# Output projection and its norm in the scheduler's order with sums in PSUM, and the last pair's convolution beside the first tiles of the down projection

## The chip, the cores and the metric

The kernel runs on one core of a Trainium2 chip. The metric is the device time of one execution in microseconds (us), median of several runs. Five engines work side by side: TensorE (PE, matmuls), VectorE (DVE), ScalarE (ACT), GpSimd (POOL), and SyncE (SP), whose queue issues most of the DMAs. Each engine works through its own instructions in order. An instruction waits until what it reads is there and what it overwrites is no longer needed.

## The reference, cut to what matters

The program is two transformer blocks on 1024 positions of width 1024, in float32. The second block is the one that the change touches:

```python
o = concat(rmsnorm_2(o_fox, fox_out_g), rmsnorm_2(o_sb, sb_out_g))   # two attentions, 512 columns each
x = x + o @ w_out
h = rmsnorm_2(x, ffn_norm_g)
u = causal_dwconv(h @ w_up, conv_w, conv_b)      # 3 taps along the positions, 2 * 2816 columns
gate, val = split(u, 2)
x = x + (silu(gate) * val) @ w_down
return rmsnorm_2(x, final_norm_g)
```

The norms are a mean of squares over the width and a reciprocal square root.

## The kernel before

Everything lies transposed: features on the 128 partitions, positions along the free dimension. A tile of the hidden state, `x2[ct]`, is 128 features by 1024 positions, with `ct` from 0 to 7. Positions are handled in two halves of 512, called A (the later half, `slice(HALF, L)`) and B.

**Matrix products.** Each float32 product is made of three products of rounded parts (`mm3`, lines 254 to 256: low by high, high by low, high by high). A weight tile is loaded into `wraw` (two buffers), ACT casts it to its high part `whi` (line 199), and POOL subtracts the two to give the low part `wlo` (line 190). `whi` and `wlo` have four buffers each. An activation is split the same way (`T` in the up projection, `rh` and `rl` in the down projection).

**Output projection.** After the attention (its loop ends at line 1123) the PSUM pool is opened anew with four banks `pp` of 128x512 and two double banks `cv` of 128x1024. The fox half of the product was added earlier, during the second attention (`x<-x,t` on POOL, `x<-xr,vec,ra` on DVE, `xr` loaded by SP). What is left is the product with the second attention's output `oh`, `ol`, four tiles of k. For `ct` 0 to 2 the products of k 0 to 2 go first, for both halves, since they don't need the last head pair; then the norm of the attention output (`half_rstd`, a matmul with `ones` and `rstd`, four DVE and two ACT instructions a half, result `rs`); then k 3. For `ct` 3 to 7 the twelve matmuls of a result go at once, all of half A first, then all of half B. `out_result` multiplies a sum by `rs`, adds it to `x2[ct]`, stores that to `x2_d`, squares it on ACT, and adds the square to `acc`. When the last A result is in, `half_rstd` gives the factor of the FFN norm for half A (`R3`); half B's follows later.

**Up projection.** It is a seven-product scheme (n from 1 to 7) on sums and differences of the four quarters of `x2` (`t_norm`, `t_sum`, `t_parts`) and of the weights (`up_sum`, `up_parts`), for 22 pairs `q` of a gate tile and a value tile. `order` lists the products; at step 1 the norm of half B is made, and `prep` puts the quarter's preparation on steps 1 to 8. `up_result` adds the products up on DVE. A pair's convolution (`up_rest(q, i)`, i from 0 to 6: two ACT instructions that start it in PSUM, four taps and two multiplications on DVE, a sigmoid on ACT) is spread over the seven products of the next pair. Its result goes to `f_d[q]` in memory. For the last pair all seven steps stand behind the last product.

**Down projection.** The pool is closed and opened with eight banks `pp`. Per group of two pairs the gated rows come back from `f_d` (`gated`, `load_split`), the weights `w_dn` are loaded in four tiles (`load_down`), and `down` adds two halves for each of eight `x2[ct]`, six matmuls a half. The `x2` tiles are reloaded from `x2_d` before the first group.

**What sets the order.** The Tile framework's scheduler orders each engine's instructions, except for those issued while `pinned[0]` is true: these keep the order in which the code is written. Pinned is everything from the start of the output projection (line 1131) to the end of the last pair's convolution.

Of the kernel before, what the change touches and what calls it, by code (L numbers as in the profile page):

```python
# [13 lines left out]
AF = mybir.ActivationFunctionType  # L14
# [83 lines left out]
def fused_blocks(ctx, tc, io, out, dbg=None):  # L98
# [126 lines left out]

    def rstd(total, r, n, scale=1.0 / D):

        v = ht("rv")[:, :n]
        t = ht("rt")[:, :n]
        pin(nc.vector.tensor_scalar(v, total, scale, EPS, op0=ALU.mult, op1=ALU.add))  # L230
        act(t, v, AF.Ln)
        act(r, t, AF.Exp, scale=-0.5)
        tt(t, r, r, ALU.mult)
        stt(t, t, -0.5, v, ALU.mult, ALU.mult)
        stt(r, t, 1.5, r, ALU.add, ALU.mult)

# [567 lines left out]
    def load_split(src, scale=None, lo=None):  # L804
        raw, hi, lo_ = ld("raw"), b1k("rh", F32R), b1k("rl", F32R)
        nc.sync.dma_start(raw, src)
        split(raw, hi, lo_, lo, scale)
        return hi, lo_
# [316 lines left out]


    log_exp_table(state["sig"])
    es.close()
    es = ExitStack()
    get = psum_pool(es, pp=(HALF, 4), cv=(L, 2))  # L1130
    pinned[0] = True
    A, B = slice(HALF, L), slice(0, HALF)
    rs["sb"], acc, R3 = b1k("rs"), b1k("acc3"), b1k("R3")

    def half_rstd(src, half, ps, r, scale):
        pin(nc.tensor.matmul(ps, ones, src[:, half], start=True, stop=True))
        rstd(ps, r[:, half], HALF, scale)

# [5 lines left out]
    def out_result(ct, half, ps):  # L1144
        x, t = x2[ct][:, half], ht("t")
        tt(t, ps, rs["sb"][:, half], ALU.mult)
        tt(x, x, t, ALU.add)
        dma(x2_d[ct][:, half], x)
        if ct == 0:
            act(acc[:, half], x, AF.Square)  # L1150
        else:
            sq = ht("sq")
            act(sq, x, AF.Square)
            tt(acc[:, half], acc[:, half], sq, ALU.add)

# [122 lines left out]
    def up_rest(q, i):  # L1278
# [16 lines left out]
        else:  # L1295
            tt(outs[q, 0], outs[q, 0], cv[q, 1], ALU.mult)
            dma(f_d[q], outs[q, 0])

    def out_load(ct):
        return load(io["w_out2"][ct, 1], 4, P)  # L1300
# [8 lines left out]
    for half in (A, B):  # L1309
        half_rstd(acc_o["sb"], half, wide[:, half], rs["sb"], 1.0 / 512)  # L1310
    for i, half in enumerate((A, B)):
# [6 lines left out]
    ws = [out_load(ct) for ct, _ in todo[:2]]  # L1318
    total = None
    for n, (ct, half) in enumerate(todo):  # L1320
        ps = get("pp")
        out_product(ps, ws[n], half, range(4))
        if n + 2 < len(todo):
            ws.append(out_load(todo[n + 2][0]))
        out_result(ct, half, ps)
        if n == 4:
            total = get("cv")
            half_rstd(acc, A, total[:, A], R3, 1.0 / D)
            for q in range(2):
                up_load(q)  # L1330
        elif n > 5:
            for k in (2 * (n - 6), 2 * (n - 6) + 1):
                t_norm(k, A)
                t_parts(1 + k // 4, k % 4)
    order = [(q, n) for n in EARLY for q in range(2)] + [(q, n) for q in range(2, NFF) for n in SEVEN]
    for q, n in order[:3]:
        up_parts(q, n)
    prep = {
        1: [(t_norm, j, B) for j in range(4)] + [(t_sum, 5, j) for j in range(4)], 2: [(t_parts, 5, j) for j in range(4)],
# [3 lines left out]
        8: [f for j in range(2, 4) for f in ((t_sum, 4, j), (t_parts, 4, j))],  # L1343
    }
    for s, (q, n) in enumerate(order):
        i = s % 7
        if s == 1:
            half_rstd(acc, B, total[:, B], R3, 1.0 / D)
        if s:
            up_result(*order[s - 1])  # L1350
        for f, *a in prep.get(s, ()):
            f(*a)
        if s == 8:
            up_load(2)
        elif q > 1 and i == 0 and q + 1 < NFF:
            up_load(q + 1)
        if i == 3 and s > 7:
            up_sum(q + 1 if q > 1 else 2, 6)
        if s + 4 < len(order):
            up_sum(*order[s + 4])  # L1360
        if s + 3 < len(order):
            up_parts(*order[s + 3])
        if q > 2:
            up_rest(q - 1, i)
        elif s >= 13:
            for i_ in ((0, 1), (2, 3), (4, 5), (6,))[(s - 13) % 4]:
                up_rest((s - 13) // 4, i_)
        up_product(q, n)
    up_result(*order[-1])
    for i in range(7):  # L1370
        up_rest(NFF - 1, i)
    pinned[0] = False
# [4 lines left out]
    get = psum_pool(es, pp=(HALF, 8))  # L1377

    def gated(grp):
        return unzip([load_split(f_d[2 * grp + kk], lo=nc.gpsimd) for kk in range(2)])  # L1380

    def down(grp, wd, c2, fh, fl, ranges=XH):
        for cc in range(2):
            ct = 2 * c2 + cc
            for ps, a, b in gemm([wd], fh, fl, ranges, c0=cc * P, per=2, ks=range(2)):
                tt(x2[ct][:, a:b], x2[ct][:, a:b], ps, ALU.add)

    def load_down(grp, c2):
        return load(io["w_dn"][grp, c2], 2, DV)

    f = gated(0)
    for ct in range(KD):
        x2[ct] = b1k("x2")
        nc.sync.dma_start(x2[ct], x2_d[ct])
    for grp in range(NFF // 2 - 1):
        nf = gated(grp + 1)
# [163 lines left out]
```

## Time and profile before

| | us |
|---|---|
| median of 3 runs | 2703.79 (2700.62 to 2707.94) |
| the profiled execution, its own time | 2703.25 |
| its span in the trace | 2701.5 |
| TensorE busy | 2507.0 (93%) |
| VectorE busy | 1614.9 (60%) |
| ScalarE busy | 1028.7 (38%) |
| GpSimd busy | 903.6 (33%) |

The page cuts the span into 40 slices of 67.5 us and gives each engine's busy share in tenths. A slice in which PE shows 5 or 6 is one in which the engine that does nearly all the work stands still for a third of the time or more. The granted clock (PEclk) is 9 or 10 tenths of full speed nearly everywhere. Where it is lower, the matmuls in that stretch ran partly at half speed. The waits list names, for an engine, which other engine's instruction ended each idle time.

### The profile page before, as it was taken

The numbers are of one execution on the slowest core, as the hardware profiler recorded it, in microseconds if no ns is written. First come the engines' busy times: TensorE is split into PE (matmuls) and PEld (weight loads), VectorE is DVE, ScalarE is ACT, GpSimd is POOL, SyncE is SP. The second block draws the span as 40 slices with busy tenths as digits, with TensorE's granted clock in tenths as the row PEclk, the third lists the DMA queues.
The fourth block names the chain that finished last, engine by engine and source line by source line (L and its number), as shares of the span: only waits on it lengthen the run. The fifth ranks groups of instructions, "written<-read, shape, count | busy, mean of one in ns | idle before, by whom it ended". The sixth has DMA issues, their size and how long they took to land. (4 is left out here: it accounts for less than half of the span.)

```text
span 2701.5 us, 36571 instructions
## 1 busy us (share of the span) xinstructions
PE 2507.0 (93%) x14126; PEld 1975.9 (73%) x14126; DVE 1614.9 (60%) x2351; ACT 1028.7 (38%) x1779; POOL 903.6 (33%) x671
## 2 busy tenths in 40 slices
PE   6989999999999999998999999996569999989996
PEld 3878968778787888877777666664347888878885
DVE  6363392766827132355666677785678777774446
ACT  4342262544634322333333434432234444453113
POOL 1433121211212224435332222231255444456423
PEclk9989999999999999999999999997789999999998
DMA  6423242433325553326444332420302222245212
GB/s 254 125 77 112 82 165 70 157 119 138 107 70 188 182 190 94 118 95 181 124 128 123 101 86 88 147 63 24 132 29 75 81 78 86 73 146 192 71 47 74
DMA packets 119629, 303.34 MB, mean 112 GB/s; under 512 B 14768, under 2 KB 19760, under 8 KB 119456
## 3 DMA queue, kind: packets, MB, share of 16 engines
q1 hardware_dynamic: 112160, 277.68, 31.0%
q0 software_dynamic: 7296, 23.34, 3.7%
q8 instruction: 111, 1.82, 0.3%
q14 instruction: 62, 0.51, 0.1%
HBM read 209.44 MB, written 87.29 MB: 110 GB/s over the span
## 5 line engine op out<-in xcount | busy, mean ns | idle before, releaser
L190 POOL TENSOR_TENSOR wlo<-wraw,whi 128x512 fp32r<-128x512 f32 (+1 forms) x280 | 414.5, 1483 | 1376.9 <-ACT whi L199 1321.6
L199 ACT CAST whi<-wraw 128x512 fp32r<-128x512 f32 (+1 forms) x280 | 172.2, 616 | 511.3 <-PE pp L256 380.7
L254 PE MATMUL pp<-hl,whi 128*128 128x512 f32 (+1 forms) x768 | 311.7, 406 | 4.4 <-DVE hl L193 4.4
L255 PE MATMUL pp<-hh,wlo 128*128 128x512 f32 (+1 forms) x768 | 306.9, 400 | 0.4 <-POOL wlo L190 0.4
L256 PE MATMUL pp<-hh,whi 128*128 128x512 f32 (+1 forms) x768 | 305.9, 398 | 0.0
L254 PE MATMUL pp<-rl,whi 128*128 128x512 f32 (+1 forms) x688 | 269.8, 392 | 7.0 <-DVE o L190 7.0
L254 PE MATMUL pp<-T,whi 128*128 128x512 f32 x616 | 246.8, 401 | 26.8 <-ACT whi L199 10.1
L256 PE MATMUL pp<-rh,whi 128*128 128x512 f32 (+1 forms) x688 | 269.7, 392 | 0.0
L255 PE MATMUL pp<-rh,wlo 128*128 128x512 f32 (+1 forms) x688 | 268.9, 391 | 0.0
L255 PE MATMUL pp<-T,wlo 128*128 128x512 f32 x616 | 246.1, 400 | 2.2 <-POOL wlo L190 2.2
L256 PE MATMUL pp<-T,whi 128*128 128x512 f32 x616 | 244.6, 397 | 0.0
L190 DVE TENSOR_TENSOR x<-x,pp 128x512 f32<-128x512 f32 (+1 forms) x184 | 121.7, 664 | 121.2 <-PE pp L256 121.2
L254 PEld LDWEIGHTS pp<-hl,whi 128*128 128x128 f32 (+1 forms) x768 | 144.7, 188 | 42.0 <-DVE hl L193 5.3
L255 PEld LDWEIGHTS pp<-hh,wlo 128*128 128x128 f32 (+1 forms) x768 | 144.6, 188 | 38.9 <-issue 6.1
L256 PEld LDWEIGHTS pp<-hh,whi 128*128 128x128 f32 (+1 forms) x768 | 144.6, 188 | 33.5 <-issue 0.4
L254 PEld LDWEIGHTS pp<-T,whi 128*128 128x128 f32 x616 | 117.3, 190 | 58.9 <-DVE T L190 11.6
L254 PEld LDWEIGHTS pp<-rl,whi 128*128 128x128 f32 x688 | 130.1, 189 | 37.1 <-issue 9.3
L190 POOL TENSOR_TENSOR wlo<-w,whi 128x512 fp32r<-128x512 f32 x88 | 115.9, 1319 | 122.4 <-ACT whi L199 122.3
L1048 DVE COPY pt<-pg 128x512 f32<-128x512 f32 (+2 forms) x192 | 101.0, 553 | 91.7 <-PE pg L1046 91.0
L256 PEld LDWEIGHTS pp<-rh,whi 128*128 128x128 f32 x688 | 130.0, 189 | 29.5 <-issue 1.7
L255 PEld LDWEIGHTS pp<-rh,wlo 128*128 128x128 f32 x688 | 130.0, 189 | 29.5 <-issue 1.3
L255 PEld LDWEIGHTS pp<-T,wlo 128*128 128x128 f32 x616 | 117.5, 191 | 30.5 <-POOL wlo L190 3.4
(380 smaller groups left out, 5515.2 us busy)
## 6 DMA issues: line engine op xcount, KB each, us to landing
w<-in_w_up SPq DMA_DIRECT2D x88, 256.0 KB
wraw<-in_w_qk SPq DMA_DIRECT2D x48, 256.0 KB
wm<-in_w_mod SPq DMA_DIRECT2D x24, 512.0 KB
wraw<-in_w_dn SPq DMA_DIRECT2D x44, 256.0 KB
f_d<-o SPq DMA_DIRECT2D x22, 512.0 KB
raw<-f_d SPq DMA_DIRECT2D x22, 512.0 KB
wraw<-in_w_out SPq DMA_DIRECT2D x37, 256.0 KB
x<-in_xT SPq DMA_DIRECT2D x16, 512.0 KB
```

Source lines behind the costliest of these rows:

```text
L190: return pin((eng or nc.vector).tensor_tensor(out=o, in0=a, in1=b, op=op))
L199: return pin(nc.scalar.copy(o, x))
L254: pin(nc.tensor.matmul(ps, ah, bl, start=first, stop=False, skip_group_check=again))
L255: pin(nc.tensor.matmul(ps, al, bh, start=False, stop=False, skip_group_check=again))
L256: pin(nc.tensor.matmul(ps, ah, bh, start=False, stop=last, skip_group_check=again))
L1048: nc.vector.tensor_copy(o, ps[:, :w])
```

## The change

1. `pinned` is set after the first three weight splits of the up projection instead of before the output projection, so the output projection, the attention's norm, the A half of the FFN norm and the preparation of half A are ordered by the scheduler.
2. `out_result` works in PSUM: the sum is multiplied by `rs` in place in its bank, and `x2` adds the bank. The squares' sum is kept in `R3`, now a double bank `cv`, instead of `acc3` in SBUF. `x2_rstd` copies half of it to SBUF (ACT), multiplies with `ones` into a `pp` bank and writes the factor back into `R3`, from which `t_norm` reads it.
3. The pinned region goes on into the down projection. At 6 products from the end the gated rows of the first two pairs are loaded and split, at 3, 2 and 1 from the end the weight tiles 0 to 2 of group 0, at 4 to 1 the `x2` tiles. Group 0's products then run in the same PSUM pool (four banks), with one step of the last pair's convolution behind each of the first seven `x2` tiles. After group 0 the eight-bank pool opens for the rest.
4. `load_split` issues its load through the helper `dma`, which can be pinned.

```diff
-    def rstd(total, r, n, scale=1.0 / D):
+    def rstd(total, r, n, scale=1.0 / D, o=None):
...
-        stt(r, t, 1.5, r, ALU.add, ALU.mult)
+        stt(r if o is None else o, t, 1.5, r, ALU.add, ALU.mult)
...
-        nc.sync.dma_start(raw, src)
+        dma(raw, src)
...
-    pinned[0] = True
...
+    def x2_rstd(half):
+
+        t = ht("acc")
+        copy(t, R3[:, half])
+        half_rstd(t, get("pp"), t, 1.0 / D, R3[:, half])
...
     def out_result(ct, half, ps):
-        x, t = x2[ct][:, half], ht("t")
-        tt(t, ps, rs["sb"][:, half], ALU.mult)
-        tt(x, x, t, ALU.add)
+        x = x2[ct][:, half]
+        tt(ps, ps, rs["sb"][:, half], ALU.mult)
+        tt(x, x, ps, ALU.add)
         dma(x2_d[ct][:, half], x)
         if ct == 0:
-            act(acc[:, half], x, AF.Square)
+            act(R3[:, half], x, AF.Square)
         else:
             sq = ht("sq")
             act(sq, x, AF.Square)
-            tt(acc[:, half], acc[:, half], sq, ALU.add)
+            tt(R3[:, half], R3[:, half], sq, ALU.add)
...
     for q, n in order[:3]:
         up_parts(q, n)
+
+    pinned[0] = True
...
         if s == 1:
-            half_rstd(acc, B, total[:, B], R3, 1.0 / D)
+            x2_rstd(B)
...
         up_product(q, n)
+        left = len(order) - s
+        if left == 6:
+            f = gated(0)
+        elif left < 4:
+            wd.append(load_down(0, 3 - left))
+        if left < 5:
+            x2_load(8 - 2 * left)
+            x2_load(9 - 2 * left)
     up_result(*order[-1])
-    for i in range(7):
-        up_rest(NFF - 1, i)
+    wd.append(load_down(0, 3))
+    for c2 in range(4):
+        down(0, wd[c2], c2, *f, step=lambda n: up_rest(NFF - 1, n) if n < 7 else None)
     pinned[0] = False
```

The order that results is read from the two built programs. On POOL, at the end of the attention, `x` are the sums with the fox half and `wlo` the low parts of the output weights. Before:

```order
L190 TENSOR_TENSOR x_2916_15972<-x_2916_15972,t_15973 128x512 x2
L190 TENSOR_TENSOR x_2943_16096<-x_2943_16096,t_16097 128x512 x2
L190 TENSOR_TENSOR x_2965_16179<-x_2965_16179,t_16180 128x512 x2
L190 TENSOR_TENSOR wlo_16229<-wraw_16227,whi_16228 128x512
L190 TENSOR_TENSOR wlo_16235<-wraw_16233,whi_16234 128x512
L190 TENSOR_TENSOR wlo_16241<-wraw_16239,whi_16240 128x512
L190 TENSOR_TENSOR wlo_16381<-wraw_16379,whi_16380 128x512
```

And after:

```order
L190 TENSOR_TENSOR wlo_16233<-wraw_16231,whi_16232 128x512
L190 TENSOR_TENSOR x_2886_15833<-x_2886_15833,t_15834 128x512 x2
L190 TENSOR_TENSOR wlo_16239<-wraw_16237,whi_16238 128x512
L190 TENSOR_TENSOR x_2916_15972<-x_2916_15972,t_15973 128x512 x2
L190 TENSOR_TENSOR wlo_16374<-wraw_16372,whi_16373 128x512
L190 TENSOR_TENSOR x_2943_16096<-x_2943_16096,t_16097 128x512 x2
L190 TENSOR_TENSOR x_2965_16179<-x_2965_16179,t_16180 128x512 x2
L190 TENSOR_TENSOR wlo_16380<-wraw_16378,whi_16379 128x512
```

The low parts of the first four output weight tiles (one more of them stands ahead of the rows shown) now stand between the attention's sums; before, the first of them stood behind the last sum. Their four casts on ACT moved in the same way, from behind the attention's last `oh` into the attention.

On DVE, the first results of the output projection (`t` and `pp` a sum times `rs`, `x` the hidden state, `acc` and `cv_16321` the sum of squares, `cv_16243` the sum of the third tile). Before:

```order
L190 TENSOR_TENSOR t_16341<-pp_16246,rs_16224 128x512
L190 TENSOR_TENSOR x_2764_15298<-x_2764_15298,t_16341 128x512
L190 TENSOR_TENSOR t_16346<-pp_16248,rs_16224 128x512
L190 TENSOR_TENSOR x_2794_15431<-x_2794_15431,t_16346 128x512
L190 TENSOR_TENSOR acc_2974_16225<-acc_2974_16225,sq_16350 128x512
L190 TENSOR_TENSOR t_16353<-cv_16245,rs_16224 128x512
L190 TENSOR_TENSOR x_2829_15570<-x_2829_15570,t_16353 128x512
L190 TENSOR_TENSOR acc_2974_16225<-acc_2974_16225,sq_16357 128x512
```

And after:

```order
L190 TENSOR_TENSOR pp_16244<-pp_16244,rs_16224 128x512
L193 SCALAR_TENSOR_TENSOR rs_16224<-rt_16314,rs_16224 128x512
L190 TENSOR_TENSOR x_2764_15298<-x_2764_15298,pp_16244 128x512
L190 TENSOR_TENSOR pp_16246<-pp_16246,rs_16224 128x512
L190 TENSOR_TENSOR cv_16243<-cv_16243,rs_16224 128x512
L190 TENSOR_TENSOR x_2794_15431<-x_2794_15431,pp_16246 128x512
L190 TENSOR_TENSOR x_2829_15570<-x_2829_15570,cv_16243 128x512
L190 TENSOR_TENSOR pp_16245<-pp_16245,rs_16224 128x512
L190 TENSOR_TENSOR cv_16321<-cv_16321,sq_16347 128x512
L190 TENSOR_TENSOR x_2764_15298<-x_2764_15298,pp_16245 128x512
L190 TENSOR_TENSOR cv_16321<-cv_16321,sq_16353 128x512
```

The addition of a square no longer stands right behind the result that it comes from, but one or two results later; and half B's first results stand among half A's.

On DVE, at the end of the up projection (`o` is a row of the last pair, `cv` its convolution, `x` with `pp` a sum of the down projection). Before:

```order
L190 TENSOR_TENSOR o_19996<-u_19957,pp_19999 128x512
L193 SCALAR_TENSOR_TENSOR cv_20042<-o_19976,vec,cv_20042 128x1023
L193 SCALAR_TENSOR_TENSOR cv_20042<-o_19976,vec,cv_20042 128x1022
L193 SCALAR_TENSOR_TENSOR cv_20044<-o_19996,vec,cv_20044 128x1023
L193 SCALAR_TENSOR_TENSOR cv_20044<-o_19996,vec,cv_20044 128x1022
L190 TENSOR_TENSOR o_19976<-o_19976,cv_20042 128x1024
L190 TENSOR_TENSOR o_19976<-o_19976,cv_20044 128x1024
L190 TENSOR_TENSOR x_3677_20071<-x_3677_20071,pp_20105 128x512
```

And after:

```order
L190 TENSOR_TENSOR o_20000<-u_19957,pp_20003 128x512
L190 TENSOR_TENSOR x_3658_19996<-x_3658_19996,pp_20082 128x512
L190 TENSOR_TENSOR x_3658_19996<-x_3658_19996,pp_20090 128x512
L190 TENSOR_TENSOR x_3659_19998<-x_3659_19998,pp_20100 128x512
L190 TENSOR_TENSOR x_3659_19998<-x_3659_19998,pp_20108 128x512
L193 SCALAR_TENSOR_TENSOR cv_20098<-o_19976,vec,cv_20098 128x1023
L190 TENSOR_TENSOR x_3665_20022<-x_3665_20022,pp_20119 128x512
L190 TENSOR_TENSOR x_3665_20022<-x_3665_20022,pp_20127 128x512
L193 SCALAR_TENSOR_TENSOR cv_20098<-o_19976,vec,cv_20098 128x1022
```

The six convolution steps that stood in a row ahead of the first down sum now stand one by one behind pairs of down sums.

## Rows read from the trace of the kernel before

**Rows 1.** The page: busy tenths in 40 slices, PE and its granted clock.

```profile
PE   6989999999999999998999999996569999989996
...
PEclk9989999999999999999999999997789999999998
```

**Rows 2.** PE's waits, 1835 to 2030 us: total, times, longest.

```profile
PE pp L254 <- ACT whi L199: 33.8, 4, 18.8
PE pp L255 <- POOL wlo L190: 11.9, 7, 5.2
...
PE cv L1136 <- DVE acc L190: 5.0, 1, 5.0
```

**Rows 3.** Stretches of 25 us: PE, PEld, DVE, ACT, POOL busy, PEclk, DMA share, GB/s.

```profile
1850.00:1875.00 25.00, 14.71 (x52) 10.53 (x51) 5.45 (x7) 6.72 (x12) 6.21 (x5) 0.63 0.03 11
1875.00:1900.00 25.00, 9.98 (x39) 6.84 (x37) 15.09 (x23) 5.67 (x9) 0.00 (x0) 0.78 0.14 52
...
1925.00:1950.00 25.00, 17.14 (x54) 12.00 (x55) 16.54 (x21) 7.82 (x13) 7.23 (x5) 0.80 0.50 170
1950.00:1975.00 25.00, 13.17 (x36) 9.05 (x35) 12.56 (x19) 8.63 (x15) 10.13 (x7) 0.65 0.21 72
1975.00:2000.00 25.00, 15.46 (x53) 11.75 (x53) 24.90 (x27) 11.24 (x21) 14.41 (x9) 0.83 0.00 0
2000.00:2025.00 25.00, 18.52 (x67) 13.17 (x66) 21.48 (x23) 8.84 (x16) 17.20 (x12) 0.90 0.07 22
```

**Rows 4.** Timeline, PE: start, us, instruction, [idle before <- releaser]; the projection's start.

```profile
1853.68 1.70 PE L1057 MATMUL pg<-pt,vt 128*64 128x128 f32 x6
1858.64 0.79 PE L254 MATMUL pp<-ol,whi 128*128 128x512 f32 x1 [3.25 <-ACT whi L199]
1864.59 0.79 PE L255 MATMUL pp<-oh,wlo 128*128 128x512 f32 x1 [5.15 <-POOL wlo L190]
...
1878.64 1.02 PE L1136 MATMUL cv<-acc_o,ones 128*128 128x512 f32 x2
```

**Rows 5.** Timeline, PE: tile 3 A, the norms of A and B, first up product.

```profile
1904.55 0.80 PE L254 MATMUL pp<-ol,whi 128*128 128x512 f32 x1 [18.79 <-ACT whi L199]
...
1928.05 2.07 PE L1136 MATMUL cv<-acc,ones 128*128 128x512 f32 x2 [5.04 <-DVE acc L190]
...
1963.73 0.79 PE L254 MATMUL pp<-T,whi 128*128 128x512 f32 x1 [10.11 <-ACT whi L199]
...
1970.96 1.02 PE L1136 MATMUL cv<-acc,ones 128*128 128x512 f32 x2
```

**Rows 6.** Timeline, DVE: the first factor `rs`, then results.

```profile
1883.20 0.69 DVE L193 SCALAR_TENSOR_TENSOR rs<-rt,rs 128x512 f32<-128x512 f32 x1
...
1887.92 0.68 DVE L190 TENSOR_TENSOR t<-pp,rs 128x512 f32<-128x512 f32 x1
...
1891.35 0.69 DVE L190 TENSOR_TENSOR acc<-acc,sq 128x512 f32<-128x512 f32 x1 [0.69 <-ACT sq L196]
...
1916.26 1.33 DVE L190 TENSOR_TENSOR acc<-acc,sq 128x512 f32<-128x512 f32 x1 [1.77 <-ACT sq L196]
```

**Rows 7.** Timeline, ACT: the cast that releases tile 3 A.

```profile
1903.88 1.25 ACT L199 CAST whi<-wraw 128x512 fp32r<-128x512 f32 x2 [2.98 <-DMA wraw<-in_w_out]
```

**Rows 8.** End of the attention: timelines of POOL and DVE, and a group of 1810 to 1856.

```profile
1797.87 4.61 POOL L190 TENSOR_TENSOR x<-x,t 128x512 f32<-128x512 f32 x2 [8.64 <-DVE x L193]
...
1799.56 1.79 DVE L190 TENSOR_TENSOR sm<-sm,sl 128x767 f32<-128x767 f32 x1
...
L190 DVE TENSOR_TENSOR sm<-sm,sl 128x767 f32<-128x767 f32 x1 | 0.9, 942 | 0.0
```

**Rows 9.** End of the up projection: timelines of PE and DVE.

```profile
2428.93 0.76 PE L254 MATMUL pp<-rl,whi 128*128 128x512 f32 x1 [7.03 <-DVE o L190]
...
2434.61 0.58 PE L255 MATMUL pp<-rh,wlo 128*128 128x512 f32 x1
...
2422.54 5.12 DVE L193 SCALAR_TENSOR_TENSOR cv<-o,vec,cv 128x1023 f32<-128x1023 f32 x4
```

More of the change, by code (lines that the diff above doesn't have):

```diff
@@ L1130, in fused_blocks, with half_rstd @@
     get = psum_pool(es, pp=(HALF, 4), cv=(L, 2))
-    pinned[0] = True
     A, B = slice(HALF, L), slice(0, HALF)
[L1133 to L1137, printed above, removed]
+    rs["sb"] = b1k("rs")
+    def half_rstd(src, ps, r, scale, o=None):
+        pin(nc.tensor.matmul(ps, ones, src, start=True, stop=True))
+        rstd(ps, r, HALF, scale, o)
+    def x2_rstd(half):
+        t = ht("acc")
+        copy(t, R3[:, half])
+        half_rstd(t, get("pp"), t, 1.0 / D, R3[:, half])
     def out_product(bank, w, half, ks):
@@ L1297, in up_rest, with gated, down, load_down @@
             dma(f_d[q], outs[q, 0])
+    def gated(grp):
+        return unzip([load_split(f_d[2 * grp + kk], lo=nc.gpsimd) for kk in range(2)])
+    def down(grp, wd, c2, fh, fl, ranges=XH, step=None):
+        for cc in range(2):
+            ct = 2 * c2 + cc
+            for ps, a, b in gemm([wd], fh, fl, ranges, c0=cc * P, per=2, ks=range(2)):
+                tt(x2[ct][:, a:b], x2[ct][:, a:b], ps, ALU.add)
+            if step:
+                step(ct)
+    def load_down(grp, c2):
+        return load(io["w_dn"][grp, c2], 2, DV)
+    def x2_load(ct):
+        x2[ct] = b1k("x2")
+        dma(x2[ct], x2_d[ct])
     def out_load(ct):
@@ L1309, in fused_blocks @@
     for half in (A, B):
-        half_rstd(acc_o["sb"], half, wide[:, half], rs["sb"], 1.0 / 512)
+        half_rstd(acc_o["sb"][:, half], wide[:, half], rs["sb"][:, half], 1.0 / 512)
+    R3 = get("cv")
     for i, half in enumerate((A, B)):
@@ L1318, in fused_blocks @@
     ws = [out_load(ct) for ct, _ in todo[:2]]
-    total = None
     for n, (ct, half) in enumerate(todo):
@@ L1326, in fused_blocks @@
         if n == 4:
-            total = get("cv")
-            half_rstd(acc, A, total[:, A], R3, 1.0 / D)
+            x2_rstd(A)
             for q in range(2):
@@ L1344, in fused_blocks @@
     }
+    wd = []
     for s, (q, n) in enumerate(order):
@@ L1377, in fused_blocks @@
     get = psum_pool(es, pp=(HALF, 8))
[L1379 to L1395, printed above, removed]
+    f = gated(1)
+    for grp in range(1, NFF // 2 - 1):
         nf = gated(grp + 1)
```

## The prediction

> **What bounds the kernel now.** I read the page's slices first: PE shows 9 tenths nearly all the way, and in the middle, after the attention, "6 5 6" with a granted clock of 7 and 8 tenths [rows 1]. This is the only long hole that the change touches. The table of stretches then shows what kind of hole it is [rows 3]. From 1850 to 1975 us PE is busy 10 to 17 of 25 us, but DVE only 5.5 to 16.5, and ACT and POOL less: no engine is full, so the time goes into waiting for one another. From 1975 to 2025 DVE is full (24.90, then 21.48 of 25). That part is bound by DVE's work, and is not made shorter by starting anything earlier in it. The waits list names the waits [rows 2]: 33.8 us for casts of weights on ACT, 11.9 us for their low parts on POOL, 5.0 us for the squares' sum. The timeline places them: 3.25 and 5.15 us at the projection's start [rows 4], 18.79 us before tile 3 of half A and 10.11 us before the first up product [rows 5]. A second, small hole is the end of the up projection: one wait of 7.03 us [rows 9].
>
> **Output projection, in steps of when something happens.** I carry the change through four events.
>
> Start. The attention's last matmuls end at 1853.68 + 1.70 = 1855.4. Before, PE then waited for a cast (3.25) and a low part (5.15) that stood behind the attention's last work on ACT and POOL [rows 4]. In the new order both stand inside the attention, so these 8.4 us go; I take 8.0, since a bank has still to be emptied. The norm's matmul moves from 1878.64 to 1870.6 [rows 4]. The first `rs` was ready at 1883.20 + 0.69 = 1883.9 [rows 6]; it would be at 1875.9, but two DVE instructions of half B now stand ahead of it (2 x 0.69), so 1877.3.
>
> Tile 3 A. Before, it started at 1904.55 after 18.79 us [rows 5], because its cast came at 1903.88, after a DMA [rows 7] whose place in SP's queue was behind the six stores of the first results. Now its weight is loaded and cast in the attention. What it needs next is a bank, free after some three DVE instructions: 1877.3 + 2.1 = 1879.4. That is 25 us earlier.
>
> Norm of half A. PE took from 1904.55 to 1928.05 - 5.04 = 1923.0 for the five A tiles, waits included, so 18.5 us; from 1879.4 it is done by 1897.9. DVE, from 1877.3: one instruction of half B's `rs`, 8 results of 2, 7 additions of squares, and ahead of the norm 3 results of half B (6) and 2 additions: 32 x 0.69 = 22.1, so 1899.4. DVE ends last. The waits on ACT's square that each result had before (0.69 [rows 6]) are filled, because the additions come later in the queue. With the new copy on ACT (one 128x512, as long as the square: about 0.63) the norm's matmul comes at 1900.0 instead of 1928.05: 28.0 us earlier.
>
> Norm of half B. Before it came 1970.96 - 1928.05 = 42.9 us after A's [rows 5], with PE waiting 10.11 in one place. DVE was busy 16.54 + 12.56 = 29.1 us in the 50 us around it [rows 3], so some 27 to 28 in the interval itself. I take DVE as the bound now: 28. Norm B then comes at 1928.0 instead of 1970.96: **43.0 us earlier**. If nothing is gained in this interval it is 28.0.
>
> After that. The preparation behind norm B is the stretch in which DVE was full [rows 3]. Its work stays, so I give it no gain. The 8 products of `x` with the factor now read PSUM; the row shows 1.33 instead of 0.69 us for a DVE instruction on SBUF while POOL worked, 0.68 for one that reads PSUM [rows 6]. Shedding such stretches might give back 0 to 5 us (8 x 0.64), and the second copy costs 0.6: I take 0, and leave 5 for the low end.
>
> [...]
>
> **What the moved casts cost.** Four casts on ACT and four low parts on POOL now lie in the attention's end, where DVE sets the pace. While POOL was busy from 1797.87 to 1802.48, DVE's 128x767 subtraction took 1.79 instead of 0.94 us [rows 8]. Each POOL instruction may stretch one such: 4 x 0.85 = 3.4 us. A cast may also wait for one of four buffers and hold up ACT's exponentials by as much again, so 0 to 7. I take 2, since POOL's new work is short beside the sums that it does there anyway, and many of DVE's instructions there read PSUM.
>
> **End of the up projection.** Removed: the wait of 7.03 us, and the slow restart. [...] That is 14 x 0.22 = 3.1 us, 10.1 in all. The conv's work on DVE stays: four taps took 5.12, 1.28 each [rows 9]. Behind a tile's two sums (0.69 each) one step makes 2.66 us of DVE for each 12 matmuls of 12 x 0.22 = 2.6 us. That is balanced to the tenth, with only four banks between them, and the first steps wait on ACT behind casts of weights that are still loading. So I expect some of the gain to be lost: 8 of 10.1, with 0 to 10 as ends. SP is passed too: eight loads of `x2`, four of gated rows and three weight tiles move ahead of the last up products, where PE needs nothing that is not already there.
>
> **Sum.** -43 + 0 + 2 - 8 = -49 against the profiled execution's 2703.25 (its span is 2701.5, and it lies 0.5 below the median of 2703.79): **2654 us**.
>
> **Rivals.**
>
> The interval between the norms doesn't shrink. DVE's preparation of half A, which before fell into DVE's idle time (20.9 of 50 us [rows 3]), now competes with half B's results, and the weights' loads, each behind a store of a result, keep their pace. Then only 28 of the 43 us come: 2654 + 15 = 2669. For it: POOL's and ACT's links are in the way as well, and two weight buffers allow no long lead. Against it: DVE was 42% idle in that interval.
>
> The boundary gives nothing: the third and fourth weight tile of group 0 wait in SP's queue behind the store of a gated row, their casts hold back the last conv on ACT, and DVE, in order, holds the sums and the four banks. The wait of 7.03 moves a few microseconds on, with its slow restart: 2654 + 8 = 2662. Both rivals together: 2677.
>
> Slower: the attention's end stalls in SP's queue. The last two loads of `xr` now stand behind weight loads, each of which waits until POOL has freed a weight buffer, and POOL's low parts stand behind sums that wait for DVE. An `xr` that comes late stops DVE, and with it every later row of the attention, one for one. It costs more than the rest brings from 51 us of delay on; with 60 it is 2712. Against it: ACT and POOL wait there most of the time (POOL 8.64 us in the row shown [rows 8]), so the buffers come free early, and nothing near 51 us is in sight.
>
> **Chances.** The forecast (2640 to 2660) 0.55; the interval 0.22; the boundary 0.12; both 0.05; slower 0.03; some smaller cost that eats nearly all, within 8 us of before, 0.03. A measurement of this kernel tells about 0.3% (8 us) from no change. Faster: 0.55 + 0.22 + 0.12 + 0.05 = 0.94, of which I give 0.02 to the same, as I have not seen the new order's waits. So 0.92, 0.05, 0.03. The range: the low end is 2654 less 5 (stretches shed), 2 (no cost in the attention), 2 (the whole boundary) and 5 for matmuls of 1950 to 2000 that now run at 0.65 and 0.83 of the clock [rows 3]: 2640. The upper end takes in both rivals: 2679. What is left out is about 0.1.
>
> **What would show it.** Right: the norm of half A some 28 us and that of half B some 43 us earlier than their distance from the attention's end was before (72.7 and 115.6 us after 1855.4), PE's waits for casts there down from 33.8 to under 10 us, no waits of PE longer than 3 us around the first down tile. DVE should be near full from the first result to the end of the preparation. Wrong: an attention that ends later by more than 5 us; a new wait of PE for a weight's DMA between the norms; or DVE's stretch of over 20 of 25 us lasting longer than before, which would mean that its work grew.

## The result and the profile after

The changed kernel takes 2657.16 us (median of 4 runs, 2653.52 to 2660.02), the kernel before 2705.57 on the same chip. The ratio is 0.9823, with a 95% interval of 0.9803 to 0.9842: 48 us less. The prediction was 2654.

The page of the changed kernel, busy tenths in 40 slices of 66.4 us (answers to [rows 1]):

```profile
PE   5989999999999999999999999998879999999996
...
PEclk9989999999999999999999999998889999999998
```

Where PE showed "6 5 6", it shows "8 8 7", and the granted clock there is 8, 8, 8 instead of 7, 7, 8 tenths. The same hole in stretches of 25 us (columns as in [rows 3]):

```profile
1850.00:1875.00 25.00, 20.39 (x82) 15.27 (x81) 9.14 (x13) 6.58 (x13) 3.15 (x3) 0.70 0.17 55
1875.00:1900.00 25.00, 20.25 (x73) 15.16 (x71) 19.89 (x29) 10.06 (x17) 8.13 (x6) 0.86 0.33 105
1900.00:1925.00 25.00, 20.32 (x77) 15.48 (x76) 17.63 (x29) 10.72 (x18) 8.78 (x7) 0.86 0.34 116
1925.00:1950.00 25.00, 15.71 (x51) 10.49 (x49) 22.95 (x31) 12.18 (x21) 11.54 (x8) 0.86 0.18 63
1950.00:1975.00 25.00, 19.22 (x58) 13.21 (x59) 22.29 (x25) 11.34 (x20) 18.68 (x12) 0.80 0.03 7
```

PE is busy 16 to 20 of 25 us where it was busy 10 to 17, and DVE 9 to 23 where it was busy 5 to 17. Both do the same work in fewer stretches. PE's waits from 1790 to 2000 us (total, times, longest; answers to [rows 2]):

```profile
PE pg L1046 <- DVE sm L190: 12.5, 6, 5.8
PE pp L1134 <- ACT acc L199: 9.0, 2, 4.7
...
PE pp L254 <- DVE x L190: 4.7, 1, 4.7
PE pp L255 <- POOL wlo L190: 3.0, 3, 2.0
```

The waits for casts of weights (33.8 us) are gone and those for their low parts are down from 11.9 to 3.0. At the top stand waits of the attention, of which this window holds more than that of [rows 2]. Behind them stands a new one: 9.0 us for the new copies on ACT, ahead of the two matmuls of the FFN norm.

Ahead of the output projection the two traces are already 3.2 us apart, in work that the change does not touch (1.5 at their first matmul, 3.1 after 174 us). So events are compared from a common mark: the group of twelve attention matmuls below, which all kernels run alike (before, then after).

```profile
1666.70 1.09 PE L1057 MATMUL pg<-pt,vt 128*64 128x128 f32 x12
```

```profile
1669.89 1.09 PE L1057 MATMUL pg<-pt,vt 128*64 128x128 f32 x12
```

The events themselves, in PE's timeline of the changed kernel: the attention's last matmuls, its norm, tile 3 A, the norms of halves A and B, the last up matmul (answers to [rows 4, 5]):

```profile
1859.56 1.70 PE L1057 MATMUL pg<-pt,vt 128*64 128x128 f32 x6
1875.44 1.02 PE L1134 MATMUL cv<-acc_o,ones 128*128 128x512 f32 x2
1886.38 0.79 PE L254 MATMUL pp<-ol,whi 128*128 128x512 f32 x1 [4.75 <-DVE x L190]
1907.83 2.07 PE L1134 MATMUL pp<-acc,ones 128*128 128x512 f32 x2 [4.68 <-ACT acc L199]
...
1934.39 2.08 PE L1134 MATMUL pp<-acc,ones 128*128 128x512 f32 x2 [4.30 <-ACT acc L199]
...
2384.24 0.40 PE L256 MATMUL pp<-T,whi 128*128 128x512 f32 x1
```

| us after the mark | before | after | moved | predicted |
|---|---|---|---|---|
| attention's end | 188.7 | 191.4 | +2.7 | +2 |
| attention's norm | 211.9 | 205.6 | -6.4 | -8 + 2 |
| tile 3 A | 237.9 | 216.5 | -21.4 | -25 + 2 |
| norm of half A | 261.4 | 237.9 | -23.4 | -28 + 2 |
| norm of half B | 304.3 | 264.5 | -39.8 | -43 + 2 |
| last up matmul | 754.8 | 714.4 | -40.4 | -43 + 2 |
| end of the span | 1034.8 | 985.7 | -49.1 | -49 |

### The profile page after: what moved, and what is told of

The parts are those of the page before. It is cut to its first block, busy times and chain, and to the rows that moved or that the text cites. A ratio compares the mean times of both kernels' runs of the same rounds, so it can differ in the third digit from the quotient of the medians.

```text
span 2655.6 us, 36554 instructions
## 1 busy us (share of the span) xinstructions
PE 2502.2 (94%) x14126; PEld 1972.9 (74%) x14126; DVE 1607.1 (61%) x2351; ACT 1028.6 (39%) x1781; POOL 905.4 (34%) x671
## 5 line engine op out<-in xcount | busy, mean ns | idle before, releaser
L190 DVE TENSOR_TENSOR x<-x,pp 128x512 f32<-128x512 f32 (+1 forms) x198 | 130.5, 664 | 110.3 <-PE pp L256 110.3
```

The lines of the kernel that those rows point to most:

```text
L190: return pin((eng or nc.vector).tensor_tensor(out=o, in0=a, in1=b, op=op))
```

## The experiments

The question was which part of the change makes which part of the 48 us, and whether the reasons hold: the order and the waits that it removes, against the sums in PSUM, which make DVE's work shorter. Ratios are to the kernel before on the same chip, with their 95% interval. From the traces I use distances from the mark: the traces of the changed kernel, of the run without part 3 and of the run without B's products agree in them to 0.2 us up to norm B.

**The boundary alone.** The kernel before with part 3:

```diff
+        left = len(order) - s
+        if left == 6:
+            f = gated(0)
...
-    for i in range(7):
-        up_rest(NFF - 1, i)
+    wd.append(load_down(0, 3))
+    for c2 in range(4):
+        down(0, wd[c2], c2, *f, step=lambda n: up_rest(NFF - 1, n) if n < 7 else None)
```

> The kernel before with part 3 of the change alone (down projection of group 0 in the pinned region, the last pair's convolution spread over it). Theory (the parts are separate, and this one removes the 7.0 us wait and the restart at half clock): 9 us less than before, no wait of PE over 1 us at the first down products, the output projection as before. Rival (the boundary's gain needs the earlier, denser stage): within 3 us of before.

Measured: 2697.41 us, ratio 0.9970 (0.9959 to 0.9981), 8 us less. PE's only wait around the first down products is 0.9 us. The part stands by itself.

**The projection alone.** The change without part 3:

```diff
...
-    wd.append(load_down(0, 3))
-    for c2 in range(4):
-        down(0, wd[c2], c2, *f, step=lambda n: up_rest(NFF - 1, n) if n < 7 else None)
+    for i in range(7):
+        up_rest(NFF - 1, i)
```

> The whole change but part 3: the end of the up projection as in the kernel before. Theory: 40 us less than before, the wait of 7 us at the first down products back, then 3 us of slow matmuls. Rival: more than 45 us less, if the new pinned region holds something back.

Measured: 2667.62 us, ratio 0.9855 (0.9839 to 0.9871), 39 us less, and the wait of 7.0 us is back. 8 and 39 make 47: the parts add up.

**Sums in SBUF.** The change with results, squares' sums and factor in SBUF, no copy:

```diff
-        tt(ps, ps, rs["sb"][:, half], ALU.mult)
-        tt(x, x, ps, ALU.add)
+        tt(t, ps, rs["sb"][:, half], ALU.mult)
+        tt(x, x, t, ALU.add)
...
-            tt(R3[:, half], R3[:, half], sq, ALU.add)
+            tt(acc[:, half], acc[:, half], sq, ALU.add)
```

> The whole change, but results, sums of squares and the FFN norm's factor in SBUF as in the kernel before (no copy on ACT either). Theory (the order makes the gain, PSUM only spares DVE the stretching beside POOL): 0 to 5 us slower than the changed kernel, so 43 to 49 less than before. Rival (the sums in PSUM make the gain, since DVE is the bound): 20 us or more slower than the changed kernel.

Measured: 2666.08 us, ratio 0.9850 (0.9827 to 0.9874). That is 7 us slower than the changed kernel by the ratios, whose intervals overlap, and 9 by the medians: more than the theory's 0 to 5, far from the rival's 20. In the traces it is 7.8 from the attention's norm to the last up matmul, of which 6.8 lie ahead of the norm of half A. From the attention's norm to the norm of half A it takes 39.2 us instead of 32.4. The groups of DVE's instructions in that stretch show why. First the run with sums in SBUF, then the changed kernel (busy us, mean ns, idle before):

```profile
L190 DVE TENSOR_TENSOR x<-x,t 128x512 f32<-128x512 f32 x11 | 13.4, 1216 | 0.1
L190 DVE TENSOR_TENSOR acc<-acc,sq 128x512 f32<-128x512 f32 x9 | 7.2, 801 | 2.9 <-ACT sq L196 2.6
```

```profile
L190 DVE TENSOR_TENSOR cv<-cv,sq 128x512 f32<-128x512 f32 x9 | 6.3, 695 | 3.0 <-ACT sq L196 2.8
...
L190 DVE TENSOR_TENSOR x<-x,pp 128x512 f32<-128x512 f32 x9 | 6.0, 676 | 0.0
L193 DVE SCALAR_TENSOR_TENSOR rs<-rt,rs 128x512 f32<-128x512 f32 x2 | 2.4, 1224 | 0.0
L193 DVE SCALAR_TENSOR_TENSOR rt<-rt,rv 128x512 f32<-128x512 f32 x2 | 2.4, 1219 | 0.0
```

The same addition takes 1216 ns with both inputs in SBUF and 676 with one in PSUM. Eleven times 0.54 is 5.9 of the 6.8 us; the nine additions of squares (801 against 695 ns) make another 0.9.

**The old order with sums in PSUM.** The changed kernel, the projection pinned again:

```diff
     get = psum_pool(es, pp=(HALF, 4), cv=(L, 2))
+    pinned[0] = True
```

> The whole change, but the output projection pinned to the order of the code as in the kernel before; sums in PSUM, new boundary. Theory (the order makes the gain): 9 us less than before from the boundary and 0 to 5 from PSUM, so 9 to 14 less; the waits for casts (18.8 and 10.1 us) still there. Rival (PSUM makes the gain): 30 or more less than before.

Measured: 2691.56 us, ratio 0.9948 (0.9931 to 0.9966), 14 us less than before. The boundary alone gave 8, which leaves 6 for PSUM, but the intervals of the two runs overlap, and the trace shows less: the last up matmul comes 3.0 us earlier than in the kernel before. The wait before tile 3 is still there, with 18.30 us. So the order is worth the other 34, and the sums in PSUM some 3 us in the old order and 8 in the new one, by the traces.

**The start alone.** The kernel before, with the first three tiles' weights and products of k 0 to 2 left to the scheduler, by setting `pinned` behind them.

> The kernel before, with only the weights and the products (k 0 to 2) of the first three output tiles left to the scheduler, the rest pinned as before. Theory (the start's two waits, 8.4 us, go, and the attention's end pays 2 to 3 for the moved casts and low parts): 6 us less than before; the attention's norm 6 us earlier, the wait of 18.8 us before tile 3 unchanged. Rival (the attention's later end is not from the moved casts): 8 us less.

Measured: 2697.66 us, ratio 0.9974 (0.9961 to 0.9986), 7 us less. The attention ends 1.5 later, its norm comes 8.5 earlier, tile 3 still waits 18.58 us for its cast, and the last up matmul is 8.0 earlier: the start's gain is passed on whole. The time does not separate the theory's 6 from the rival's 8. That the moved tiles do cost the attention time is shown in the section on the prediction.

**The change without its start.** The changed kernel, that first part pinned:

```diff
+    pinned[0] = True
     three = [out_load(ct) for ct in range(3)]
...
             out_product(b, w, half, range(3))
+    pinned[0] = False
```

> The whole change, but the same first part pinned in the order of the code, so that the four casts and low parts stand behind the attention again. Theory: the attention ends 2.7 us earlier than in the changed kernel, PE waits 8 us more at the start, so 6 us slower than the changed kernel, 42 less than before. Rival (a later start is hidden, since DVE is the bound behind it): same as the changed kernel within 2 us.

Measured: 2662.98 us, ratio 0.9850 (0.9832 to 0.9867), 6 us slower than the changed kernel by the medians and 7 by the ratios, near the theory's 6. The norm of the attention comes 6.8 us later and the last up matmul 7.0: a later start isn't hidden.

**Without the copy.** The last addition of a half's squares writes to SBUF:

```diff
-        t = ht("acc")
-        copy(t, R3[:, half])
+        t = last[half.start]
...
+            if ct == KD - 1:
+                o = last[half.start] = ht("acc")
```

> The whole change, but the last addition of a half's squares writes to SBUF, so ACT's copy goes. PE waited 4.7 and 4.3 us for the copies. Theory (DVE's last addition ends only some 1.4 us before the matmul, so the copy is worth its own time and one hand-over): both norms 1 to 1.5 us earlier, 2 to 3 us faster than the changed kernel. Rival (the copy is the wait): 9 us faster.

Measured: 2652.00 us, ratio 0.9808 (0.9792 to 0.9824), 4 to 5 us faster than the changed kernel. From the attention's norm to the last up matmul the trace gains 3.0 us, which is the theory's 2 to 3. Its parts are others: the norm of half A comes 1.2 us earlier from there, as forecast, but the interval between the norms shrinks by 3.4, and 1.5 of that are lost again behind norm B. Another 2.6 us of the trace lie before the attention's norm, where the order is the same; the paragraph on the clock below tells of them. The rival is out: PE's wait of 4.7 us before norm A only changed its name, to 4.05 for DVE's addition. That of 4.3 before norm B fell to 1.0, since the copy for B stood on ACT behind two casts and began 2.0 us after its input was there, as ACT's and DVE's rows of the changed kernel show:

```profile
1932.57 1.28 ACT L199 CAST T<-x 128x512 fp32r<-128x512 f32 x2 [1.49 <-DVE x L193]
1933.76 0.58 ACT L199 COPY acc<-cv 128x512 f32<-128x512 f32 x1
```

```profile
1931.07 0.69 DVE L190 TENSOR_TENSOR cv<-cv,sq 128x512 f32<-128x512 f32 x1
```

**The factors' chains in PSUM.** That kernel, with the temporary of `rstd` in the bank of the norm:

```diff
-        t = ht("rt")[:, :n]
+        t = ht("rt")[:, :n] if t is None else t
...
-        rstd(ps, r, HALF, scale, o)
+        rstd(ps, r, HALF, scale, o, ps)
```

> As the run without the copy, and the factors' chains (Ln, Exp, square, two products) keep their temporary in the norm's PSUM bank. Theory (VectorE is stretched beside POOL only where both operands are in SBUF; three instructions of 1.67 to 1.77 us fall to 0.7): 3 us faster than the run without the copy. Rival (the stretch has another cause, or the bank is held longer and holds up a product): no gain or up to 3 us slower than that run.

Measured: 2648.22 us, ratio 0.9795 (0.9779 to 0.9811), 4 us faster than the run without the copy; 3.4 in the trace from the attention's norm to the last up matmul. Two products of the chains in the changed kernel, then one in this run, each with POOL's row beside it:

```profile
1881.09 1.77 DVE L193 SCALAR_TENSOR_TENSOR rs<-rt,rs 128x512 f32<-128x512 f32 x1
1882.79 1.75 DVE L193 SCALAR_TENSOR_TENSOR rt<-rt,rv 128x512 f32<-128x512 f32 x1
1881.03 2.95 POOL L190 TENSOR_TENSOR wlo<-wraw,whi 128x512 fp32r<-128x512 f32 x2 [11.84 <-ACT whi L199]
```

```profile
1877.73 0.69 DVE L193 SCALAR_TENSOR_TENSOR rs<-cv,rs 128x512 f32<-128x512 f32 x1
1877.79 2.51 POOL L190 TENSOR_TENSOR wlo<-wraw,whi 128x512 fp32r<-128x512 f32 x2 [10.87 <-ACT whi L199]
```

One instruction of the chain still has both inputs in SBUF, the square of half B, and that one still takes 1.40 us beside POOL in this run. The whole traces differ by 4.1 us, but other things are in that: the run without the copy comes to the mark 3.2 us later (1670.76 against 1667.58), and needs 2.7 us less from there to the attention's norm (202.9 against 205.6). The 3.4 us are the figure to go by.

**Two tiles early.** That kernel, where the casts of the third and fourth tile are held back until the attention's last square on ACT:

```diff
...
-    three = [out_load(ct) for ct in range(3)]
+    three = [out_load(ct, state["osq"] if ct == 2 else None) for ct in range(3)]
...
-    ws = [out_load(ct) for ct, _ in todo[:2]]
+    ws = [out_load(ct, state["osq"]) for ct, _ in todo[:2]]
```

> As the run with the chains in PSUM, but the casts and low parts of the third and fourth output tile stand behind the attention's last square again, those of the first two stay in the attention. Theory (in the changed kernel the cast of the third tile waits 3.0 us on ACT for a buffer, in front of the attention's exponentials; two tiles are 36 matmuls and cover the third's cast and low part): the attention ends 1.5 to 2.5 us earlier, no new wait at the projection's start, 1.5 to 2.5 us faster than that run. Rival (the attention's later end comes from the low parts on POOL or the loads, not from this cast): under 1 us.

Measured: 2645.47 us, ratio 0.9789 (0.9774 to 0.9804), the fastest kernel of the study: 3 us under the run before it by the medians, though the intervals overlap. The third tile's cast no longer waits; in the changed kernel it did, on ACT:

```profile
1824.35 0.62 ACT L199 CAST whi<-wraw 128x512 fp32r<-128x512 f32 x1 [3.04 <-issue]
```

The attention ends 1.7 us earlier than in the run before it, as the theory said, but not for that cast. In the two traces the attention's matmuls lie within 0.1 us of each other up to 168 us after the mark, 14 us behind it: that wait was covered. The run before falls back by 1.1 us only then, where POOL makes the low part of the fourth tile beside DVE's work for the attention, and by another 0.5 up to the end. So the rival's reason, the low parts on POOL, is the one that the traces show; the rows stand in the section on the prediction. From the attention's norm on the two traces differ by only 0.2 us.

**Less work on DVE behind norm B.**

```diff
-        1: [(t_norm, j, B) for j in range(4)] + [(t_sum, 5, j) for j in range(4)],
+        1: [(t_sum, 5, j) for j in range(4)],
...
-        3: [(t_norm, j + 4, B) for j in range(4)] + [(t_sum, 7, j) for j in range(4)],
+        3: [(t_sum, 7, j) for j in range(4)],
```

> The changed kernel, leaving out the eight products of half B with its norm's factor (t_norm of B), which DVE makes behind norm B, 5.4 us in the trace of the changed kernel. Theory (DVE bounds the stretch behind norm B): 4 to 5.5 us faster than the changed kernel. Rival (PE waits there for ACT's casts or POOL's low parts, DVE is only busy): under 1.5 us faster.

Measured: 2654.83 us, ratio 0.9818 (0.9804 to 0.9831), 2 us faster than the changed kernel by the medians and 1.4 by the ratios; the last up matmul comes 1.3 us earlier, although 5.4 us of DVE's work are gone. The theory fell, and the rival's figure came: DVE's throughput does not bound that stretch.

**Low parts from POOL to DVE.** My next theory was that POOL bounds it. On the kernel with two tiles early, behind norm B, all low parts on DVE, or three of four:

```diff
-        split(src, t[:, :HALF], t[:, HALF:], nc.gpsimd if j % 2 else None)
+        split(src, t[:, :HALF], t[:, HALF:], nc.gpsimd if j % 2 and n < 3 else None)
```

> As the run with two tiles early, but behind norm B all low parts of the up projection's activations are made on DVE; POOL made every second one (10 of 20, 1.3 us each). The run without B's products fell short, so DVE alone is not the bound there. Theory (POOL is: it holds 20 of 25 us with weights' and activations' low parts, and each of its instructions stretches one of DVE's by about 1 us, more than the 0.69 that the low part costs on DVE): 1 to 4 us faster than that run. Rival (DVE is the bound after all): 10 x 0.69, so 3 to 7 us slower.

> As that run, but POOL keeps every fourth low part (5 of 20). Theory: between the two, 0.5 to 3 us faster than the run with two tiles early. If the best balance lies between, faster than both neighbours.

Measured: 2650.13 us (0.9797, 0.9780 to 0.9815) and 2649.44 us (0.9793, 0.9776 to 0.9809), 4 to 5 us slower than the kernel with two tiles early by the medians, and within the intervals by the ratios; the last up matmul comes 4.7 and 2.7 us later. Both theories fell, so POOL isn't the bound either. The rival's figure came (3 to 7 us), yet its reason is not right: with all low parts on DVE, DVE was busy 62.4 us of the 75 behind norm B, and 66.8 with half of them. Its low parts, first in the run with two tiles early, then with all on DVE:

```profile
L190 DVE TENSOR_TENSOR T<-x,T 128x512 fp32r<-128x512 f32 x12 | 12.8, 1085 | 3.4 <-ACT T L199 3.4
```

```profile
L190 DVE TENSOR_TENSOR T<-x,T 128x512 fp32r<-128x512 f32 x22 | 15.7, 747 | 5.8 <-ACT T L199 5.8
```

Ten more instructions cost only 2.9 us more, since each became shorter: POOL was busy 29.8 of the 75 us instead of 48.9. What PE waited for is seen in DVE's timeline of that run (start, us, instruction, idle before):

```profile
1955.97 0.69 DVE L190 TENSOR_TENSOR x<-x,x 128x512 f32<-128x512 f32 x1
1957.40 0.69 DVE L190 TENSOR_TENSOR T<-x,T 128x512 fp32r<-128x512 f32 x1 [0.74 <-ACT T L199]
1958.01 0.68 DVE L190 TENSOR_TENSOR x<-x,x 128x512 f32<-128x512 f32 x1
1959.43 0.69 DVE L190 TENSOR_TENSOR T<-x,T 128x512 fp32r<-128x512 f32 x1 [0.74 <-ACT T L199]
```

The code writes difference, cast, low part for one quarter and then for the next. In this order DVE makes a difference, waits 0.74 us for ACT's cast of it, makes the low part, and only then the next difference. Where POOL made every second low part, one such wait of two was not DVE's. PE waited 8.22 us in one piece for a row `o` that DVE made behind this chain. So I take it that what bounds the stretch is, at least in these steps, the pinned order of a chain over two engines, and not how full an engine is. That is read from these rows and not shown by a run: an order with the four differences ahead of the four casts was not tried.

## Why the prediction was right, and where it was not

**The four events.** All came within 3 us of the forecast, and the last up matmul within 1 (table above). The first rival, that the interval between the norms keeps its 42.9 us, is out: 1934.39 - 1907.83 = 26.6 us. But the forecast owes part of its closeness to errors that cancelled.

- Start. Between the attention's end and its norm 9.1 us went (23.3 us before, 14.2 after) where I had 8.0. The granted clock in the 15 us from 190 us after the mark was 0.83 instead of 0.61. That made up for the attention's later end.
- Tile 3 A came 1.6 us later than forecast. I had priced the chain of the factor at 0.69 an instruction ("2 x 0.69"), but two of its products, whose inputs lie in SBUF, took 1.77 and 1.75, about 2.1 us more. The run with the chains in PSUM gained 2.3 us between the attention's norm and norm A.
- Norm of half A came 2.6 us later. In the step "32 x 0.69" two errors cancel. The waits on ACT's squares were not all filled: 2.8 us of them are left (the row of `cv<-cv,sq` above). In return DVE's instructions there start 0.60 us apart where nothing holds them, and not 0.69.
- Norm of half B. Forecast 28 us for the interval, with DVE as the bound; measured 26.6, and DVE was busy for only 20.5 of them. The number was luck. My figure for DVE's work was too high to begin with (25.3 us in that interval before, not 27 to 28), and DVE did not set the pace. At its end PE waited 4.30 us for the copy, which I had put at 0.6; without the copy the interval is 23.2 us, with DVE busy for 17.2.

**Signs.** Of the signs that I had named, DVE "near full from the first result" did not show: it was busy 19.89 and 17.63 of 25 us there. And one sign of being wrong did show: DVE was busy for over 20 of 25 us in four stretches on end (from 1925 to 2025 us: 22.95, 22.29, 21.68, 22.21) where it had been in three (24.90 and 21.48 [rows 3], then 22.29). DVE's work had not grown: over the execution it was 1607.1 us instead of 1614.9. The sign did not measure what I meant it to.

**Sums in PSUM.** I put what reading PSUM spares at 0, and looked for it behind norm B. There it spared 2.0 us (449.8 us from norm B to the last up matmul, against 451.8 with the sums in SBUF). The larger part, 6.8 us, came ahead of norm A, where I had priced all 32 instructions at 0.69 [rows 6]. That is what an instruction took with an input in PSUM (676 ns) or with POOL idle (0.69 us [rows 6]); with the sums in SBUF the order alone would have given less than I forecast, by 7 us. The row for the right reading was there: 1.33 us for an addition of a square while POOL worked [rows 6]. The runs with sums in PSUM were faster than their twins, by 7 us and by 3 to 6, and the rows of DVE beside POOL show the same sign: 1216 against 676 ns.

**The attention's end.** Forecast +2, measured +2.7. Of the two mechanisms put forward one is there: a low part on POOL stretches an instruction of DVE, and PE waits for it. Two such places make 1.9 of the 2.7 us. DVE's scan beside the second low part takes 3.06 instead of 2.28 us, and its subtraction beside the fourth 3.48 instead of 2.41, for which PE then waits 5.82 instead of 4.74. After (POOL, DVE, PE), then before:

```profile
1812.43 1.28 POOL L190 TENSOR_TENSOR wlo<-wraw,whi 128x512 fp32r<-128x512 f32 x1 [6.64 <-ACT whi L199]
1812.80 3.06 DVE L1009 TENSOR_TENSOR_SCAN sl<-sl,zerot 128x1024 f32<-128x1024 f32 x1
1842.16 1.57 POOL L190 TENSOR_TENSOR wlo<-wraw,whi 128x512 fp32r<-128x512 f32 x1
1841.06 3.48 DVE L190 TENSOR_TENSOR sm<-sm,sl 128x383 f32<-128x383 f32 x2
1844.69 1.51 PE L1046 MATMUL pg<-ident,sm 128*128 128x128 f32 x6 [5.82 <-DVE sm L190]
```

```profile
1809.49 2.28 DVE L1009 TENSOR_TENSOR_SCAN sl<-sl,zerot 128x1024 f32<-128x1024 f32 x1
1836.82 2.41 DVE L190 TENSOR_TENSOR sm<-sm,sl 128x383 f32<-128x383 f32 x2
1839.38 1.51 PE L1046 MATMUL pg<-ident,sm 128*128 128x128 f32 x6 [4.74 <-DVE sm L190]
```

So 0.8 and 1.1 us, near the 0.85 that I took from [rows 8], in two of four places. In the run with two tiles early the subtraction is back at 2.41 and PE's wait at 4.73, while the second low part, which stayed, still stretches the scan. The other mechanism, a cast that waits (3.04 us) and holds up ACT's exponentials, cost next to nothing: behind the third cast the traces of the changed kernel and of that run are still within 0.2 us. The slower rival, 51 us from late loads of `xr`, found nothing.

**Behind norm B.** "Its work stays, so I give it no gain" came out (the last up matmul gained 0.6 more than norm B), but the reason, that DVE bounds the stretch by its work, was wrong: 5.4 us of that work could go for a gain of 1.3. A share of 24.90 of 25 us [rows 3] was read as a full engine. It holds instructions that are stretched by POOL (nine of its 27 took 1.64 to 1.78 us). What sets the pace where they are not is, as I read the rows with all low parts on DVE, the chain; no run has shown it.

**The boundary.** Forecast 8 of 10.1, measured 8 alone, and in the whole change 49.1 - 40.4 = 8.7 in the traces. No run shows the 0.22 us that stand in the forecast's 14 x 0.22 and 12 x 0.22; it was my estimate, half of 0.44. In the trace before, the thirteen distances from 2428.93 to 2434.61 [rows 9] are 0.44 us in the mean at a granted clock of 0.50, and from 2436 us on the matmuls come 0.23 apart at 1.00; the changed kernel has 0.23 at 1.00 in its first down products too. So the restart cost 14 x 0.21 = 2.9 us and not 3.1, and twelve matmuls of a step take 2.8 us and not 2.6. The second rival's mechanism occurred on a small scale, and the banks absorbed it. ACT, then DVE, then PE of the changed kernel:

```profile
2392.83 0.62 ACT L199 CAST whi<-wraw 128x512 fp32r<-128x512 f32 x1 [1.66 <-DMA wraw<-in_w_dn]
2393.36 2.34 ACT L196 ACTIVATE cv<-o,vec 128x1024 f32<-128x1024 f32 x2
```

```profile
2394.59 1.29 DVE L193 SCALAR_TENSOR_TENSOR cv<-o,vec,cv 128x1023 f32<-128x1023 f32 x1 [3.68 <-ACT cv L196]
```

```profile
2396.62 0.47 PE L254 MATMUL pp<-rl,whi 128*128 128x512 f32 x1 [0.88 <-DVE x L190]
```

The cast of the fourth weight tile waited for its DMA, the convolution's start behind it on ACT came late, and DVE stood for 3.68 us with sums queued behind it. PE had four banks to fill meanwhile and lost 0.88.

## What to carry to other kernels

Follow a change of order through the few events that must happen one after the other, and price each by the engine that is last there; here this gave 49 for 48 us, in part by errors that cancelled, where adding up the waits in the list (33.8 + 11.9 + 5.0 + 7.0) would have promised more. Compare the engine's busy time in each interval with its length before you call it the bound. Price instructions of VectorE by where their inputs lie and whether POOL is busy then (here 1216 against 676 ns for one addition), and move a temporary into a PSUM bank that is free anyway (here worth 3.4 us). A busy share near 100% in an order that is fixed by hand is no proof of a full engine (here 5.4 us of DVE's work went for a gain of 1.3): take some work away before you build on it.

## What the runs showed of the hardware

In the changed kernel's trace VectorE's additions and products of 128x512 with both inputs in SBUF took up to 1.1 us longer beside POOL, 1.64 to 1.79 us instead of 0.69, also with the output in PSUM: the last product of the factor writes to PSUM from two SBUF inputs and takes 1668 ns; an addition and a product with one PSUM input, in the same stretches, take 676 to 738:

```profile
L193 DVE SCALAR_TENSOR_TENSOR x<-x,vec,cv 128x512 f32<-128x512 f32 x8 | 5.4, 738 | 0.0
...
L193 DVE SCALAR_TENSOR_TENSOR cv<-rt,acc 128x512 f32<-128x512 f32 x1 | 1.7, 1668 | 0.0
```

Which of the two started first made the difference. In that trace 47 such two-input instructions were running when POOL's began: they took 685 ns in the mean, none over 693. Of 70 that began with more than 0.8 us of POOL's instruction still to come, 51 took 1.64 to 1.79 us and ended some 0.55 us after POOL's. The other 19 lay beside POOL instructions that were themselves 2.2 to 11.3 us long instead of 1.3. I read these lengths as one waiting for the other and not as two sharing; no run tests that. Of 205 instructions with an input in PSUM that ran beside POOL none took over 754 ns.

The same attention, in the same order, comes at two times, and that goes with the clock. At 103 us after the mark the granted clock falls from 1.00 to 0.50 for 3.4 us in the changed kernel's trace, while PE waits 1.34 us for DVE; in the run without the copy PE waits as long there and the clock stays at 1.00. From 100 to 110 us after the mark, changed kernel, then the run without the copy (columns as in [rows 3]):

```profile
1769.89:1779.89 10.00, 8.65 (x54) 6.29 (x55) 6.51 (x9) 2.14 (x6) 6.45 (x6) 0.83 0.56 144
```

```profile
1770.76:1780.76 10.00, 8.66 (x59) 6.03 (x59) 7.65 (x11) 3.49 (x8) 6.45 (x6) 1.00 0.56 152
```

From there on the second trace is 1.3 us ahead, and 1.6 at the attention's end. PE's eight `pg<-ident,sm` at that place take 1.06 us in the run without the copy, and 1.94 in nine others: those of the kernel before, the changed kernel, the start alone, the change without its start, the chains in PSUM, two tiles early, less work on DVE, and the two with low parts moved. Three traces end the attention early for their order: that of the boundary alone at 187.6 us after the mark, against 188.7 to 189.0 in the old order, and those of the sums in SBUF and of the run without the copy at 189.8, against 191.4 in the new one with all its tiles moved. What decides on the drop is open. With the norm behind it, which comes 2.6 us earlier, it is worth as much as some of the effects measured here, so differences of this size were taken from the stretch behind that norm.
